# Second heads with queries on partitions in thirteen units instead of eight, value offset 66, four outputs kept in DRAM

## The chip, the cores and the metric

The kernel runs on one core of a Trainium2 chip. The metric is the device time of one execution in microseconds. Before the change three runs took 1343.99 to 1344.94 us, median 1344.91.

A core has TensorE (PE, with weight loads shown apart as PEld), VectorE (DVE), ScalarE (ACT), GpSimd (POOL), SyncE (SP, which here only issues transfers) and 16 DMA engines. Each engine runs its own instructions in order and waits on semaphores for the others.

## The reference

Two layers over 1024 latent tokens and 256 context tokens of width 1024, 16 heads of 64. The first layer is grouped-query attention (four key/value heads, per-head norm and rotary positions on q and k) over all 1280 keys; the second is neighbourhood attention. Each layer's input projection also yields a gate. Cut to what the change touches:

```python
def gqa_axial_mixer(hx, hc, w_in, q_g, k_g, w_out, cos, sin, need_ctx_out):
    ...
    def block(qi):
        s = jnp.einsum('bqkgd,bskd->bkgqs', qi, k_all).astype(jnp.float32) * ATTN_SCALE
        p = jax.nn.softmax(s, axis=-1).astype(v_all.dtype)
        return jnp.einsum('bkgqs,bskd->bqkgd', p, v_all)
    ...
    yx = (o * jax.nn.silu(z)) @ w_out
```

All of it is in float32. The kernel carries float32 operands as two float16 parts (high and low) and makes three products of them: high by high, high by low, low by high.

## The kernel before, in words

**Stages.** First come modulation, norms and the k and v projections (0 to about 95 us). Then the first layer's attention goes over eight pairs of heads. A pair's q and gate projection (`a_proj`) runs about one pair ahead of its attention, in five blocks of two token tiles: `mm` is the 48 matmuls of a block (L1034) with norm, rotation and split, `post` transposes q, `mgen` finds each query's maximum score, `rows` puts the negated maximum into a row of `q2`. Then come the first layer's output projection (`a_out`, L1358), the second layer's pairs (`b_proj`, `b_att`), and its output projection (L1739).

**Two forms of attention.** A unit here is one head of one pair for one half (four tiles) of the latent tokens. There are 32 units; `pt_` 0 and 1 are the halves, and 2 is the context's queries.

- The k form, `a_att`: scores stand with keys on partitions (L1260, L1261), ten tiles of 128x512 a unit. Queries' maxima must be known ahead: `mgen` computes the scores once more, with queries on partitions (L1068 for the latent keys, L1074 for the context), and DVE reduces them (L1069, L1075). ACT takes the exponential twice, to float16 and to float32 (L1245, L1247), `p_split` makes the low part (POOL, every sixth time DVE, L1127 to L1130), and `pv_mm` multiplies by values: three matmuls per tile (L1136 to L1138), whose 65th column sums the probabilities.
- The q form, `q_att`: scores stand with queries on partitions (L1186, L1187), one pass on DVE copies them and takes the maximum (L1190), ACT takes the exponentials (L1202, L1203; the second also sums), and a DMA transpose (L1205) brings the probabilities' two parts to keys on partitions. The products are two matmuls per tile: L1211 multiplies the high part by both value parts, 128 columns, and L1213 the low part by the high values, 64 columns. The two halves of the result are added at the end, and sums are applied by DVE (L1222 to L1229). No `mgen` is needed.

Before the change the q form serves the second head of pairs 0 to 3, in both halves: `QH = range(0, 4)`, eight units. The other 24 have the k form.

**Values.** `v1` (and `bv1` in the second layer) holds, per key tile and head, 130 float16 numbers: 64 high parts, a constant for the sums at 64, 64 low parts from 65, one unused. L1137 and, in the second layer, L1648 read the low parts, `65:129`.

**Buffers.** `y_tile` gives tiles of two rotating sets of four, Y0 and Y1. Outputs `oa` of pairs 0 to 3 stay in Y0, of pairs 4 to 7 in Y1. The q form's probabilities and their transposes (`qpp`) rotate in Y1 too, so they can be there only while pairs 4 and on have no output yet. The output projection's buffers (`opool`) lie where those of the q projection (`aj`) were. The output weights lie where the normed tokens (`xh`) were.

**Order.** Generators with start and end times in units of a pair (`timeline`) write the program's order. Then `Planner` builds the graph of all instructions, gives each a cost per engine, schedules them by list, refines five times with due times and fixes each engine's order. It computes no results; a price in it changes orders alone. DMA transfers are issued by SP in its order.

Of the kernel before, what the change touches and what calls it, by code (L numbers as in the profile page):

```python
# [36 lines left out]
QH = range(0, 4)  # L37
# [5 lines left out]
class Planner:  # L43
# [72 lines left out]
    def cost(self, x, rd, wr):  # L116
# [173 lines left out]
    def schedule(self, key=None, margin=0.0, scale=None):  # L290
# [65 lines left out]
        while count < N:  # L356
# [43 lines left out]
            if e == "PE":  # L400
# [55 lines left out]
    def deadlines(self, margin):  # L456
# [4 lines left out]
        for a in self.order["PE"]:  # L461
            idle += max(0.0, start[a] - prev)
            prev = max(prev, start[a] + (cst[a][0] if tuple(self.node[a].tile_size or (128, 128))[1] == 128
                                         else cst[a][0] / 4))
# [35 lines left out]
def timeline(items):  # L500

    live = [[g, float(a), (float(b) - a) / tot, 0.0] for g, a, b, tot in items]
    while live:
        it = min(live, key=lambda e: e[1] + e[2] * e[3])
        try:
# [4 lines left out]
            live.remove(it)  # L510

# [12 lines left out]
def trunk_kernel(ctx, tc, x, cx, cc, norm_g, ng_row, b_cols, sel_c, w_m0, w_mb, b_mod, a_wkv, a_wq, a_qg, a_kg, a_w_out,  # L524
# [242 lines left out]
    v1 = ap.tile([P, NT, NKV, 130], F16, name="v1")  # L767
# [240 lines left out]

    FTAG = ("pj", "pj", "st", "pj", "pj")

    def a_proj(u, at):
# [3 lines left out]
        def mm(b):  # L1015
            wt = wa[u]
            pt_ = b // 2
            if b % 2 == 0:
# [4 lines left out]
                     [aq.tile([P, 4, 3], F32, name=f"mxp{u}{pt_}{i}", tag=f"mxp{i}", bufs=3) if i == 0 or pt_ == 2 or u not in QH  # L1023
                      else None for i in range(2)])
                if pt_ < 2 and u in QH:
# [34 lines left out]
        def mgen(b):  # L1060
            q1, _, _, mxs = pairs[(u, b // 2)]
            g = u // 2
            for i in ((0,) if b < NX // 2 and u in QH else (0, 1)):
# [14 lines left out]
        def rows(pt_):  # L1078
            q2, mxs = pairs[(u, pt_)][1], pairs[(u, pt_)][3]
            n = PTN[pt_]  # L1080
            for i in ((0,) if pt_ < 2 and u in QH else (0, 1)):
# [7 lines left out]
        for b in range(NT // 2):  # L1089
            m = (1100 if u in QH else 2200) if b < 4 else 440  # L1090
            if u == 0:
                v, w, vp, vm, mw = FIRST[b]
            else:
                v = at + 0.2 * b
                d = 0.2 * (b in (0, 2))
                w, vp, vm, mw = 0.2, v + 0.29 + d, v + 0.31 + d, 0.2 * m / (1100 if u in QH else 2200)
            items.append((mm(b), v, v + w, 5120))
            items.append((post(b), vp, vp + 0.01, 220))
            items.append((mgen(b), vm, vm + mw, m))
            if b in (1, 3, 4):  # L1100
                items.append((rows(b // 2), vm + mw + 0.01, vm + mw + 0.02, 400))
# [30 lines left out]
    def pv_mm(pv, hi, lo, v, n, first, last):  # L1132

        for t in range(n):
            c = slice(t * P, (t + 1) * P)
            T.matmul(pv[:, t, :], hi[:, c], v[:, 0:65], start=first and t == 0, stop=False)  # L1136
            T.matmul(pv[:, t, 0:HD], hi[:, c], v[:, 65:129], start=False, stop=False)  # L1137
# [15 lines left out]

    og_t, og_n = {}, {}
# [6 lines left out]
    def og_done(u, pt_):  # L1161

        og_n[(u, pt_)] = og_n.get((u, pt_), 0) + 1
        if og_n[(u, pt_)] == 2:
            og = og_t[(u, pt_)]
            if pt_ < 2:
                o_out(aq, og, 4, o_dst("oa", oa, u)[:, 4 * pt_:4 * pt_ + 4], u, f"{u}{pt_}")
            else:
                o_out(aq, og, 2, oc[:, u], u, f"{u}c")

    def q_att(u, pt_):
# [5 lines left out]
        sums = aq.tile([P, 4, 3], F32, name=f"qsm{u}{pt_}", tag="qsm", bufs=2)  # L1177
        og = og_of(u, pt_)
        for t in range(4):
# [17 lines left out]
            for c, (k0, n) in enumerate(KCH):  # L1197
# [5 lines left out]
                S.activation(pf, pf, AF.Exp, bias=nmx, accum_out=sums[:, t, c:c + 1])  # L1203
# [3 lines left out]
                def pvs(ppt=ppt, k=k, k0=k0, t=t):  # L1207
                    for x_ in range(k):
                        kt = k0 // P + x_
                        vv = v1[:, kt, g, :].rearrange("p (a b) -> p a b", b=65)[:, :, 0:HD]  # L1210
                        T.matmul(pv[:, t, :].rearrange("p (a b) -> p a b", b=HD), ppt[:, x_], vv,  # L1211
                                 start=t == 0 and kt == 0, stop=False)
                        T.matmul(pv[:, t, 0:HD], ppt[:, k + x_], v1[:, kt, g, 0:HD], start=False,  # L1213
# [7 lines left out]
        sm = aq.tile([P, 4], F32, name=f"qse{u}{pt_}", tag="qse", bufs=2)  # L1221
        V.tensor_reduce(sm, sums, axis=AX.X, op=ALU.add)  # L1222
        V.tensor_scalar_mul(sm, sm, 2.0 * WS * WS)
        V.reciprocal(sm, sm)
        qo = aq.tile([P, 4, HD], F32, name=f"qoc{u}{pt_}", tag="qoc", bufs=1)
# [7 lines left out]
    def a_att(u, pt_):  # L1233
# [19 lines left out]
        for i in ((0,) if pt_ < 2 and u in QH else (0, 1)):  # L1253
# [591 lines left out]
```

## Time and profile before

| | |
|---|---|
| median of three runs | 1344.91 us |
| profiled execution | 1345.52 us |
| its span, first to last instruction | 1343.7 us |
| mean granted TensorE clock | 0.992 |
| first layer's pairs and output projection | about 95 to 785 us |
| second layer's pairs | about 820 to 1288 us |

The profile is of one execution. A row of a group gives line, engine, operation, output and inputs by the program's names, shapes and count, then busy time, the mean ns of one, and the idle time before. Matmuls overlap, so the mean ns of one is longer than what it costs; the timeline shows the starts. Windows give, for each stretch, its length, each engine's busy time with its count of instructions, the granted clock, the DMA engines' busy share and GB/s. A row of a transfer gives size and time from issue to landing.

### The profile page before, as it was taken

What the parts mean: (1) busy time and instruction counts of PE and PEld (TensorE: products, weight loads), DVE (VectorE), ACT (ScalarE), POOL (GpSimd) and SP (SyncE); (2) the same over time, 40 slices, a digit from 0 to 9 for tenths busy, and PEclk for the clock granted to TensorE, in tenths of its full rate; (3) what the DMA queues carried; (4) which work ended last, traced back from release to release, by engine and by line L of the source; (5) the groups of instructions that cost most, each with busy time, mean ns of one, the idle gap of its engine ahead of it and who ended that gap; (6) DMA issues with size and microseconds to landing.
All of it is one profiled execution on the core that took longest, in us unless ns stands there. A gap on an engine that the chain in (4) does not pass through costs nothing.

```text
span 1343.7 us, 38645 instructions
## 1 busy us (share of the span) xinstructions
PE 1309.6 (97%) x15100; PEld 928.6 (69%) x15100; DVE 1067.1 (79%) x2456; ACT 969.0 (72%) x2076; POOL 891.2 (66%) x1214
## 2 busy tenths in 40 slices
PE   8999999999999999999999989999999999999996
PEld 4457777777777777776654457869687786968552
DVE  5898787888889787769528997878888888887665
ACT  4554889988888777798743456878878888887453
POOL 2323878777777767687876467677676868767543
PEclk9899999999999999999999999999999999999998
DMA  9633576786675222244317962678777877669952
GB/s 371 188 116 96 111 152 117 145 187 135 140 145 122 74 67 72 59 119 108 113 51 187 243 139 82 125 145 152 150 139 142 158 143 162 145 151 226 286 130 110
DMA packets 390496, 191.64 MB, mean 143 GB/s; under 512 B 349792, under 2 KB 355104, under 8 KB 390312
## 3 DMA queue, kind: packets, MB, share of 16 engines
q1 hardware_dynamic: 389736, 189.13, 62.1%
q8 instruction: 118, 1.93, 0.6%
q14 instruction: 66, 0.54, 0.1%
q10 hardware_dynamic: 576, 0.03, 0.0%
HBM read 91.03 MB, written 15.75 MB: 79 GB/s over the span
## 4 chain that ended last, share of the span: by engine, by line
PE 73%; DVE 10%; ACT 6%; DMA 5%; issue 3%; POOL 2%; DVEq 0%; POOLq 0%; SPq 0%; ACTq 0%
PE pa L1034 13%; PE poa L1358 6%; PE pob L1739 6%; PE st L1260 3%; PE st L1261 3%; PE pm L1068 3%; PE pkv L887 2%; PE pv L1137 2%; PE pv L1138 2%; PE pv L1136 2%; DMA bpht<-bph 2%; DMA qpp<-qpp 2%; PE pvc L1577 1%; PE qpv L1211 1%; PE pbc L1527 1%
## 5 line engine op out<-in xcount | busy, mean ns | idle before, releaser
L1130 POOL TENSOR_TENSOR pl<-pf,ph 128x256 f16<-128x256 f32 x400 | 274.9, 711 | 85.7 <-ACT pf L1247 56.2
L1130 POOL TENSOR_TENSOR bph<-bpf,bph 128x256 f16<-128x256 f32 (+1 forms) x224 | 184.0, 848 | 102.0 <-ACT bpf L1637 81.8
L1034 PE MATMUL pa<-wa,x 128*128 128x256 f16 x1536 | 219.8, 272 | 0.7 <-DVE q L822 0.7
L1245 ACT ACTIVATE ph<-st 128x512 f16<-128x512 f32 x240 | 143.8, 602 | 58.0 <-PE st L1261 56.2
L1565 PEld LDWEIGHTS <-hx 128*128 128x128 f16 x2688 | 157.3, 98 | 10.2 <-issue 1.3
L1034 PEld LDWEIGHTS <-x 128*128 128x128 f16 x1536 | 140.4, 97 | 33.3 <-issue 1.4
L1247 ACT ACTIVATE pf<-st 128x512 f32<-128x512 f32 x240 | 143.6, 604 | 2.0 <-DVE pl L1127 0.9
L1069 DVE TENSOR_REDUCE mxp<-pm 128x1 f32<-128x512 f32 x192 | 127.3, 683 | 12.8 <-PE pm L1068 11.7
L1137 PE MATMUL pv<-v,ph 128*128 128x64 f16 x960 | 122.4, 195 | 0.0
L1136 PE MATMUL pv<-v,ph 128*128 128x65 f16 x960 | 121.9, 193 | 0.2 <-ACT ph L1245 0.2
L1138 PE MATMUL pv<-v,pl 128*128 128x65 f16 x960 | 121.3, 192 | 0.0
L1130 POOL TENSOR_TENSOR qpp<-qpf,qpp 128x256 f16<-128x256 f32 (+1 forms) x158 | 93.4, 616 | 31.6 <-ACT qpf L1203 29.3
L1517 PEld LDWEIGHTS <-wb 128*128 128x128 f16 x672 | 63.9, 98 | 71.9 <-issue 6.6
L1635 ACT ACTIVATE bph<-bpf,bnx 128x384 f16<-128x384 f32 (+1 forms) x128 | 69.3, 581 | 52.4 <-DVE bnx L1627 33.8
L1136 PEld LDWEIGHTS <-ph 128*128 128x128 f16 x960 | 90.9, 97 | 22.1 <-ACT ph L1245 0.7
L1137 PEld LDWEIGHTS <-ph 128*128 128x128 f16 x960 | 90.4, 97 | 15.8 <-issue 0.4
L1138 PEld LDWEIGHTS <-pl 128*128 128x128 f16 x960 | 91.2, 99 | 9.3 <-POOL pl L1130 1.2
L1260 PE MATMUL st<-q,k 128*128 128x512 f16 x240 | 90.8, 379 | 0.7 <-ACT pf L1247 0.4
L1261 PE MATMUL st<-q,k 65*128 65x512 f16 x240 | 91.5, 381 | 0.0
L1358 PE MATMUL poa<-woa,oa 128*128 128x512 f16 x384 | 89.8, 379 | 0.0
L1739 PE MATMUL pob<-wob,obf 128*128 128x512 f16 x336 | 80.5, 379 | 1.9 <-DVE acc L1742 1.4
L1434 POOL TENSOR_TENSOR wtb<-wsb 128x256 f32<-128x256 f32 x64 | 56.5, 884 | 32.5 <-DMA wsb<-in_b_wp 17.0
(485 smaller groups left out, 4050.2 us busy)
## 6 DMA issues: line engine op xcount, KB each, us to landing
wg<-in_w_mb SPq DMA_DIRECT2D x32, 512.0 KB, 4.5
wsb<-in_b_wp SPq DMA_DIRECT2D x64, 256.0 KB, 2.8
wm<-in_w_m SPq DMA_DIRECT2D x16, 512.0 KB, 9.0
wsa<-in_a_wq SPq DMA_DIRECT2D x32, 256.0 KB, 3.5
xstage<-in_x SPq DMA_DIRECT2D x8, 512.0 KB, 5.6
wsoa<-in_a_w_out SPq DMA_DIRECT2D x16, 256.0 KB, 2.7
x<-in_x SPq DMA_DIRECT2D x8, 512.0 KB, 8.5
x_d<-x SPq DMA_DIRECT2D x8, 512.0 KB, 5.1
```

Of the source, the lines that this page charges most:

```text
L1034: T.matmul(ps[:, :, i, :], hA(a, kt, t), wt[w][:, kt, :], start=n == 0, stop=n == 3 * KT - 1)
L1130: G.tensor_tensor(lo[:, c], p32[:, c], hi[:, c], op=ALU.subtract)
L1136: T.matmul(pv[:, t, :], hi[:, c], v[:, 0:65], start=first and t == 0, stop=False)
L1137: T.matmul(pv[:, t, 0:HD], hi[:, c], v[:, 65:129], start=False, stop=False)
L1138: T.matmul(pv[:, t, :], lo[:, c], v[:, 0:65], start=False, stop=last and t == n - 1)
L1245: S.activation(ph, st, AF.Exp)
L1247: S.activation(p32, st, AF.Exp)
L1260: T.matmul(so, k1[:, g, kc], q1[:, :, i, :], start=True, stop=False)
L1261: T.matmul(so, k2[0:65, g, kc], q2[0:65, :, i, :], start=False, stop=True)
L1358: T.matmul(ps, lhs(a, kt), w[b][:, kt, :], start=n == 0, stop=n == 3 * KT - 1)
L1565: T.matmul(ps[:, t * P:(t + 1) * P], hx[a][:, t, blk, kt], wt[j][:, s_, w, kt], start=first and t == 0 and m == 0, stop=last and t == 3 an ...
L1739: T.matmul(ps, ob[kt][:, t, a], wout["b"][hf][b][:, kt, :], start=n == 0, stop=n == 3 * len(kts) - 1)
```

## The change

- The q form serves the second head of pairs 0 to 6 in the first half and of pairs 0 to 5 in the second half: thirteen units for eight. The predicate is `in_q(u, pt_)`.
- In the q form the products are three matmuls per tile as in the k form, 65, 64 and 65 columns, the sums come from the 65th column, and `o_evict` writes the result. The accumulator of the second exponential and the steps L1222 to L1229 are gone.
- All `oa` tiles are of Y0. Those of pairs 0 to 3 are stored to DRAM (`oa_d`) after their second half and loaded into Y1 (`oa_back`) at 6.98, just ahead of the output weights.
- The rows of values are 132 long, and low parts start at 66.
- Pair 7's projection is spread by a table `LATE` from 6.0 to 7.33, before 6.0 to 7.0. The maxima of its second head follow apart from those of its first.
- In the planner the least price of a matmul is 30.4 ns, 140 for float32 with under 8 columns, and a matmul on 32 columns of the array occupies PE for 0.3 of its cost.

```diff
-QH = range(0, 4)
+QH = (7, 6, 0)
...
-            return max(cols * passes / 2.4 + 2.5, 29.0), 170.0
+            return max(cols * passes / 2.4 + 2.5, 140.0 if f32 and cols < 8 else 30.4), 170.0
...
-                    t[e] = s + 7
+                    t[e] = s + 0.3 * occ
...
+def in_q(u, pt_):
+    return u < QH[pt_]
...
-    v1 = ap.tile([P, NT, NKV, 130], F16, name="v1")
+    v1 = ap.tile([P, NT, NKV, 132], F16, name="v1")
...
-        V.tensor_tensor(v1[:, t, :, 65:129], vv, v1[:, t, :, 0:HD], op=ALU.subtract)
+        V.tensor_tensor(v1[:, t, :, 66:130], vv, v1[:, t, :, 0:HD], op=ALU.subtract)
...
-            d[u] = y_tile((P, NX, 2, P), F16, f"{kind}{u}", u // 4)
+            d[u] = y_tile((P, NX, 2, P), F16, f"{kind}{u}", 0)
...
+    LATE = ((0.0, 0.25, 0.5, 0.66, 0.1, 0.9), (0.3, 0.25, 0.64, 0.76, 0.1, 1.0), (0.7, 0.25, 1.1, 1.3, 0.05, 1.45), (0.97, 0.23, 1.28, 1.36, 0.05, 1.52), (1.1, 0.2, 1.34, 1.38, 0.05))
...
+        late = u == NPAIR - 1
+
+        def heads(pt_):
+            return (0,) if in_q(u, pt_) or late and pt_ < 2 else (0, 1)
...
+            elif late:
+                v, w, vp, vm, mw = (z + at * (n in (0, 2, 3)) for n, z in enumerate(LATE[b][:5]))
...
+            if late and b < 4:
+                vm = at + LATE[b][5]
+                items.append((mgen(b, (1,)), vm, vm + mw, 1100))
+                if b % 2:
+                    items.append((rows(b // 2, (1,)), vm + mw + 0.01, vm + mw + 0.02, 400))
...
-            T.matmul(pv[:, t, 0:HD], hi[:, c], v[:, 65:129], start=False, stop=False)
+            T.matmul(pv[:, t, 0:HD], hi[:, c], v[:, 66:130], start=False, stop=False)
...
+    oa_d = dram.tile([NPAIR // 2, P, NX * 2 * P], F16, name="oa_d")
+
+    def oa_back():
+        for u in range(NPAIR // 2):
+            oa[u] = y_tile((P, NX, 2, P), F16, f"oar{u}", 1)
+            DM.dma_start(oa[u].rearrange("p t a q -> p (t a q)"), oa_d[u])
...
+                if pt_ and u < NPAIR // 2:
+                    DM.dma_start(oa_d[u], oa[u].rearrange("p t a q -> p (t a q)"))
...
-                S.activation(pf, pf, AF.Exp, bias=nmx, accum_out=sums[:, t, c:c + 1])
+                S.activation(pf, pf, AF.Exp, bias=nmx)
...
-                        vv = v1[:, kt, g, :].rearrange("p (a b) -> p a b", b=65)[:, :, 0:HD]
-                        T.matmul(pv[:, t, :].rearrange("p (a b) -> p a b", b=HD), ppt[:, x_], vv,
-                                 start=t == 0 and kt == 0, stop=False)
-                        T.matmul(pv[:, t, 0:HD], ppt[:, k + x_], v1[:, kt, g, 0:HD], start=False,
+                        T.matmul(pv[:, t, 0:65], ppt[:, x_], v1[:, kt, g, 0:65], start=t == 0 and kt == 0, stop=False)
+                        T.matmul(pv[:, t, 0:HD], ppt[:, x_], v1[:, kt, g, 66:130], start=False, stop=False)
+                        T.matmul(pv[:, t, 0:65], ppt[:, k + x_], v1[:, kt, g, 0:65], start=False,
...
-        S.copy(qo, pv[:, :, HD:P])
-        V.tensor_tensor(qo, pv[:, :, 0:HD], qo, op=ALU.add)
-        for t in range(4):
-            V.scalar_tensor_tensor(og[:, t, HD:P], qo[:, t], sm[:, t:t + 1], sz[:, t, HD:P], op0=ALU.mult, op1=ALU.mult)
+        o_evict(aq, pv, og, 4, sz, 0, 1, f"q{u}{pt_}")
...
+    items.append((once(oa_back), 6.98, 6.99, 1))
...
-        v1_ = bq.tile([P, NT, 2, 130], F16, name=f"bv1{u}", tag="v1")
+        v1_ = bq.tile([P, NT, 2, 132], F16, name=f"bv1{u}", tag="v1")
...
-                                T.matmul(pv[:, t % 4, 0:HD], pht[:, x_], v1_[:, kt, i, 65:129], start=False, stop=False)
+                                T.matmul(pv[:, t % 4, 0:HD], pht[:, x_], v1_[:, kt, i, 66:130], start=False, stop=False)
```

More of the change, by code (lines that the diff above doesn't have):

```diff
@@ L1058, in post, with mgen @@
             yield 220
-        def mgen(b):
+        late = u == NPAIR - 1
+        def heads(pt_):
+            return (0,) if in_q(u, pt_) or late and pt_ < 2 else (0, 1)
+        def mgen(b, ii):
             q1, _, _, mxs = pairs[(u, b // 2)]
             g = u // 2
-            for i in ((0,) if b < NX // 2 and u in QH else (0, 1)):
+            for i in ii:
                 if b < NX // 2:
@@ L1076, in mgen, with rows @@
                 yield 220
-        def rows(pt_):
+        def rows(pt_, ii):
             q2, mxs = pairs[(u, pt_)][1], pairs[(u, pt_)][3]
             n = PTN[pt_]
-            for i in ((0,) if pt_ < 2 and u in QH else (0, 1)):
+            for i in ii:
                 zm = zmax[nrow[0] % len(zmax)]
@@ L1252, in a_att @@
         og = og_of(u, pt_)
-        for i in ((0,) if pt_ < 2 and u in QH else (0, 1)):
+        for i in ((0,) if in_q(u, pt_) else (0, 1)):
             pvs = ps_pv(f"pv{u}{i}{pt_}")
@@ L1313, in trunk_kernel @@
     for u in range(NPAIR):
[L1314 removed]
+        for pt_, v, c in ((0, u, 16800 - 8000 * in_q(u, 0)), (1, u + PSH, 16800 - 8000 * in_q(u, 1)), (2, u + 2 * PSH, 2400)):
             items.append((a_att(u, pt_), v, v + (PSH if pt_ < 2 else 1 - 2 * PSH), c))
[L1316 removed]
+            if in_q(u, pt_):
                 items.append((q_att(u, pt_), v - QLEAD, v + PSH - QLEAD, 4 * 1925 + 500))
```

25 lines of the change are left out of this document (9 added, 16 removed).

## The prediction

> **What bounds the kernel now.** I read the page's busy line and its chain first.
>
> ```profile
> span 1343.7 us, 38645 instructions
> PE 1309.6 (97%) x15100; PEld 928.6 (69%) x15100; DVE 1067.1 (79%) x2456; ACT 969.0 (72%) x2076; POOL 891.2 (66%) x1214
> PE 73%; DVE 10%; ACT 6%; DMA 5%; issue 3%; POOL 2%; DVEq 0%; POOLq 0%; SPq 0%; ACTq 0%
> ```
>
> PE is busy for 97% of the span and is 73% of the chain that ended last. A share of busy time is a mean over stages, so the second view is the windows. I cut them where every 240th matmul of the first layer's projection (L1034) starts, because a pair has 240 of them. The first row below is for those matmuls alone and shows one pair's 240. The others are for all instructions, with PE, PEld, DVE, ACT and POOL busy, granted clock and DMA share.
>
> ```profile
> 478.80:553.20 74.40, 36.44 (x240) 21.38 (x240) 1.00 0.29 67
> ...
> 192.20:262.90 70.70, 69.65 (x911) 54.40 (x910) 59.41 (x175) 64.45 (x151) 54.78 (x85) 1.00 0.73 140
> 262.90:332.90 70.00, 68.50 (x868) 52.61 (x865) 59.38 (x169) 61.20 (x144) 51.36 (x78) 1.00 0.77 159
> 332.90:401.50 68.60, 68.24 (x849) 52.31 (x849) 58.53 (x163) 57.62 (x137) 53.05 (x84) 1.00 0.72 145
> 401.50:478.80 77.30, 76.78 (x1044) 58.40 (x1043) 62.80 (x145) 62.90 (x133) 55.05 (x83) 1.00 0.40 91
> 478.80:553.20 74.40, 74.34 (x1011) 56.33 (x1010) 55.33 (x118) 55.61 (x112) 53.21 (x76) 1.00 0.29 67
> 553.20:624.40 71.20, 71.20 (x943) 54.36 (x942) 58.54 (x120) 58.95 (x120) 54.30 (x75) 1.00 0.33 91
> 624.40:690.00 65.60, 64.14 (x775) 38.40 (x773) 33.45 (x70) 48.99 (x95) 52.69 (x73) 1.00 0.34 97
> 690.00:820.00 130.00, 125.54 (x884) 69.13 (x881) 110.43 (x168) 55.74 (x102) 79.72 (x88) 0.99 0.69 168
> 820.00:1288.00 468.00, 462.21 (x5925) 349.06 (x5923) 382.92 (x873) 367.16 (x788) 335.35 (x438) 1.00 0.79 161
> ```
>
> The three windows from 192.2 to 401.5 have the second head with queries on partitions. They last 70.7, 70.0 and 68.6 us, mean 69.8. The three from 401.5 to 624.4 do not, and last 77.3, 74.4 and 71.2, mean 74.3. PE is busy for nearly all of every one, at a granted clock of 1.00, and so it is in the second layer (820 to 1288). ACT is next, at 55 to 64 us. So both attention stages are paid in PE time: what an edit is worth there is how long PE's stream becomes, as long as ACT, DVE, POOL and DMA keep up. Five more units (a unit is one head, half the tokens, one pair) take the form of the shorter windows, where two units are of that form. The windows alone say (74.3 - 69.8) / 2 = 2.3 us a unit, 11.3 us for five, stalls included.
>
> **The change part by part.** A matmul's own duration is no price: matmuls overlap. The price is the distance from one start to the next in the timeline of PE.
>
> ```profile
> 251.26 0.27 PE L1034 MATMUL pa<-wa,xc_hi 128*128 128x256 f16 x1
> 251.37 0.27 PE L1034 MATMUL pa<-wa,xc_lo 128*128 128x256 f16 x1
> ...
> 251.54 0.19 PE L1136 MATMUL pv<-v,ph 128*128 128x65 f16 x1
> 251.57 0.19 PE L1137 MATMUL pv<-v,ph 128*128 128x64 f16 x1
> 251.61 0.19 PE L1138 MATMUL pv<-v,pl 128*128 128x65 f16 x1
> 251.64 0.19 PE L1136 MATMUL pv<-v,ph 128*128 128x65 f16 x1
> 251.66 0.20 PE L1137 MATMUL pv<-v,ph 128*128 128x64 f16 x1
> 251.70 0.19 PE L1138 MATMUL pv<-v,pl 128*128 128x65 f16 x1
> 251.73 0.19 PE L1136 MATMUL pv<-v,ph 128*128 128x65 f16 x1
> ...
> 252.00 0.38 PE L1186 MATMUL qs<-k,q 128*128 128x512 f16 x1
> 252.22 0.22 PE L1211 MATMUL qpv<-v,qpp 128*128 128x128 f16 x1
> 252.28 0.19 PE L1213 MATMUL qpv<-v,qpp 128*128 128x64 f16 x1
> 252.30 0.22 PE L1211 MATMUL qpv<-v,qpp 128*128 128x128 f16 x1
> ...
> 252.56 0.38 PE L1187 MATMUL qs<-k,q 65*128 65x512 f16 x1
> 252.78 0.19 PE L1136 MATMUL pv<-v,ph 128*128 128x65 f16 x1
> ```
>
> So 512 columns take 0.22 us, 256 take 0.11, 128 take 0.06. From 251.54 to 252.00 stand five triples of value products: 92 ns each. From 252.22 to 252.56 stand four pairs of the other form: 85 ns each. Within the triples L1137, with 64 columns, takes about 35 ns, while L1136 and L1138, with 65, take 30 or less; L1213, also 64 columns, takes 20 to 30. L1137 reads from element 65 of a row of 130 two-byte values, an odd place. The others start at an even one.
>
> ```profile
> L1137 PE MATMUL pv<-v,ph 128*128 128x64 f16 x960 | 122.4, 195 | 0.0
> L1138 PEld LDWEIGHTS <-pl 128*128 128x128 f16 x960 | 91.2, 99 | 9.3 <-POOL pl L1130 1.2 <-issue 0.5
> L1648 PE MATMUL bpv<-bv,bpht 128*128 128x64 f16 x608 | 69.1, 195 | 0.0
> L1203 ACT ACTIVATION_READ_ACCUMULATOR qpf<-qpf,qnx 128x1 f32 x96 | 19.2, 200 | 0.0
> oa<-oo SPq DMA_TRANSPOSE x14, 3.1
> acc<-x_d SPq DMA_DIRECT2D x8, 512.0 KB, 6.4
> x<-in_x SPq DMA_DIRECT2D x8, 512.0 KB, 8.5
> ```
>
> *Maxima of five units go.* A unit's maximum pass is 8 matmuls of 512 columns, 4 of 256 and 4 of 128 (the row of maxima): 8 x 0.22 + 4 x 0.11 + 4 x 0.06 = 2.44 us. Five units: -12.2 us. The scores cost the same in either form: twice 10 x 512 columns a unit. The DVE reductions go too, and a pass over the scores that also takes the maximum comes instead; DVE is at 55 to 63 us in windows of 68 to 77 and stays beside PE.
>
> *Value products of the q form: three instructions for two.* The 320 tiles that had this form go from 85 ns to a triple of 30 + 30 + 28 = 88: +1.0 us. The 200 tiles of the moved units go from 92 to 88: -0.8 us. Together about 0.
>
> *Value offset 66 and row 132.* It touches L1137 in what stays of the k form (19 units x 40, and 64 for the context: 824) and L1648 of the second layer (608): 1432 matmuls. If odd starts are the cause, each goes from about 34 to about 29: 1432 x 5 ns = -7.2 us. The ends are 0 (something else makes L1137 slow) and 1432 x 6 = -8.6. I take -7.2, since the only thing in which L1213 differs that should matter is the start.
>
> *ACT and DVE of the q form.* The accumulator reads (19.2 us in all) and a copy and six small DVE operations a unit go; a reciprocal and two multiplications come. All lies beside PE: 0. Were that cover gone, it would be a gain of some 2 us a unit.
>
> *Stalls that the q form brings.* Time less PE busy is 1.05, 1.50 and 0.36 in its windows, mean 0.97, against 0.52, 0.06 and 0.00, mean 0.19: 0.4 us a unit, +2.0 us for five. The moved units issue 12 transposes each on SP, 24 a pair as in the earlier windows, whose DMA share of 0.72 to 0.77 and whose SP queue bear it; so pairs 4 and 5 go from about 0.3 to that.
>
> *Outputs via DRAM.* Four stores and four loads of 512 KB, at about 6.4 us each (row of acc). A store on SP waits for its transpose to land (3.1 us); behind it on SP are weight loads and transposes with buffers ahead. Four such waits, 12 us spread over 280: 0. The loads wait until the last probabilities of pair 6 give up their buffers. They are due 0.42 of a pair (29 us) ahead of the first output projection and take 4 x 6.4 = 26 us if one after another: just covered, 0. Uncovered, the price is up to 26 us. Nothing excludes that it shifts other transfers for the better by the 1.5 us that PE idles from 624 to 690.
>
> *Last pair stretched.* About 2.5 of its five projection blocks (48 x 0.11 = 5.3 us each) and two of its maximum units go from pair 6's window to pair 7's. Pair 6 then has 71.2 - 13 - 5 = 53 us of PE work, against ACT's 58.95 less 2.9 for those blocks, 56. So up to 3 us of stall there unless PE draws on later work; in pair 7 PE gets 82 us against ACT's 52 and stays the bound. Ends 0 and +3, and as a gain the 1.5 us of idle time that is there; I take +2, near the upper end, since the row of pair 6 shows no slack to give. With each block go its ACT and DVE steps, a power on POOL behind the splits of probabilities there, and a transpose and copies on SP, now among the loads of output weights. The output projection's buffers lie where the projection's were, so its residual rows (8.5 us) come only after the last block; the two PSUM banks give PE 10 us of output products meanwhile (2 x 24 x 0.22) and attention fills the rest: 0.
>
> *Planner's prices.* They only change orders. The second layer idles 5.8 us in 468, so a better order can win at most that, and a worse one lose about as much: 0.
>
> Sum: -12.2 - 7.2 + 2.0 + 2.0 = -15.4. The profiled execution took 1345.5 us (span 1343.7), 0.6 above the median of the runs. So 1345.5 - 15.4 = 1330.1, and as a median about 1329.5 us.
>
> **Rivals.** *The offset does nothing.* L1137 would be slow because its weights are those of L1136 again. For it: the same repetition stands in L1648. Against it: it would have to spare the other loads. Time: 1329.5 + 7.2 = about 1337.
>
> *The read-back comes late.* Its place is the start of the output projection near 640 us. The four loads sit on SP in order, ahead of output weights and residual rows, behind buffers that pair 6 must give up. If these buffers come free when PE already needs the tiles, PE waits: four loads one after another, 26 us, less what attention of pair 7 fills. From 15 us of exposed wait the change is slower than before; at the full 26 it ends at 1355. For it: the next 54 us of PE are output projection alone. Against it: 29 us of lead, and loads overlap on 16 DMA engines at a share of 0.34 there.
>
> *Weight loads bind the third product.* Each of the three loads its own weights, and the loads' row says 99 ns. If that could not hide, 320 tiles would pay 99 ns more, 32 us, and the time would be about 1369 with the offset gone too. Against it: three products with three loads take 92 ns together, at 251.54 to 252.00, so loads overlap. The Trainium skill states for such streams, in "TensorE: Matmul & The Clock Gate", section "Back-to-back issue gap", about 81 ns per 128-column matmul with its load; by that the 320 tiles would pay 26 us, and with no gain from the offset the sum would be 1363, slower. The trace disagrees: 92 ns for three.
>
> *The orders and the stretched pair eat the gain.* If pairs 4 to 7 idle as the passage between the layers does (4.5 us in 130) and the second layer doubles its 5.8, some 13 us go: within 0.2% of before, 1343.
>
> **How the numbers follow.** Forecast 0.68; offset without effect 0.16, still faster; orders eat the gain 0.04; late read-back 0.11; weight loads 0.01. A measurement tells from no change what differs by over 0.2%, here 2.7 us. Faster 0.84, same 0.04, slower 0.12. The likeliest case runs from -12.2 - 8.6 - 1.5 with no new stall (1322.6) to 1332.5 with all of pair 6's and twice the stalls of the q form. The range goes 2.6 lower for better orders, and above it takes in the rival at 1337 with 3 us of worse ones: 1320 to 1340, which leaves out late read-back and most of what the orders eat.
>
> **What would show it.** L1068 count 152 for 192 and L1108 108 for 128; pair windows of 68 to 71 us for pairs 4 and 5, with ACT near 60 and a DMA share of 0.7; the start after each L1137 and L1648 coming 28 to 30 ns later; second layer shorter by about 3 us; no PE wait that names the read-back tiles. Wrong it becomes if PE waits on DMA at the first output projection, if pairs 6 and 7 together last longer than their PE work, or if the 64-column products keep their 34 ns.

## The result and the profile after

The changed kernel takes 1353.73 us (median of five runs, 1352.31 to 1360.46) against 1344.91 before: a ratio of 1.0072, 95% interval 1.0049 to 1.0095. It is 9 us slower where 15 us faster was forecast. The profiled execution took 1354.29 us. The first lines of its page:

```profile
span 1352.5 us, 39348 instructions
PE 1304.3 (96%) x15360; PEld 922.4 (68%) x15360; DVE 1071.8 (79%) x2523; ACT 970.2 (72%) x1987; POOL 893.8 (66%) x1235
```

PE is busy 5.3 us less than before, in a span that is 8.8 us longer. Its work did fall; what grew is the time in which it stands still. The windows show where. First the kernel before, then the changed one, in the first layer's attention: window, length, then PE, PEld, DVE, ACT and POOL busy, granted clock, DMA share and GB/s.

```profile
95.00:406.00 311.00, 306.30 (x3740) 237.85 (x3738) 261.73 (x731) 254.07 (x590) 222.49 (x339) 1.00 0.67 137
406.00:551.00 145.00, 144.82 (x1980) 109.78 (x1979) 112.65 (x245) 112.03 (x233) 104.53 (x153) 1.00 0.34 77
551.00:695.00 144.00, 142.54 (x1797) 98.05 (x1795) 94.07 (x196) 112.16 (x222) 110.81 (x152) 1.00 0.33 92
```

```profile
95.00:406.00 311.00, 302.65 (x3977) 234.24 (x3976) 242.98 (x674) 241.44 (x485) 219.70 (x338) 0.99 0.73 140
406.00:551.00 145.00, 140.38 (x1939) 107.27 (x1936) 113.78 (x322) 119.79 (x238) 107.20 (x164) 1.00 0.77 148
551.00:695.00 144.00, 137.08 (x1768) 94.02 (x1767) 104.03 (x229) 112.58 (x225) 110.61 (x159) 1.00 0.55 129
```

PE's idle time in the three goes from 4.7, 0.2 and 1.5 us (together 6.35) to 8.4, 4.6 and 6.9 (19.9): 13.5 us more. The first window holds the value products of the same seven and a half units of the q form in both kernels, the second about four of the new ones, the third the last. So 3.7 of the 13.5 us came where no unit is new. What PE waits for in this stretch, before and after (who waited for what: us in total, times, longest):

```profile
PE qpv L1211 <- DMA qpp<-qpp: 0.9, 2, 0.7
```

```profile
PE qpv L1237 <- DMA qpp<-qpp: 9.3, 16, 1.5
PE st L1278 <- ACT pf L1265: 4.2, 7, 1.8
PE pm L1079 <- issue: 2.1, 1, 2.1
```

The first value product of the q form now waits for the transpose of its probabilities. The scores of the k form wait until ACT has read the buffer that they go to.

These waits count only gaps that the modelled ends of matmuls leave open. A finer measure is the distance from each start of PE to the next, less the median for a matmul of its line and form, where it is longer than that; added up I call it stall. From 95 to 695 us the stall is 32.7 us before and 50.9 after.

A small part of this is the clock. Here is one window before and after (the clock is the third number from the end):

```profile
263.00:335.00 72.00, 70.50 (x892) 54.42 (x889) 61.01 (x177) 63.20 (x149) 53.46 (x82) 1.00 0.78 160
```

```profile
263.00:335.00 72.00, 69.37 (x924) 52.45 (x921) 56.66 (x160) 56.66 (x113) 51.14 (x78) 0.98 0.86 160
```

An estimate of its worth is 0.02 of 72 us, 1.4 us of the 18.2. Over the whole execution the clock was 0.994 in this profile and 0.992 before, so it does not explain the 9 us.

The matmuls of the first layer's output projection, before and after, with first and last start (the last two numbers):

```profile
L1358 PE MATMUL poa<-woa,oc x96: 378/380/380, 753.5 to 774.0; 128*128 128x512 f16 x96
```

```profile
L1376 PE MATMUL poa<-woa,oar x192: 377/379/380, 646.0 to 756.5; 128*128 128x512 f16 x192
L1376 PE MATMUL poa<-woa,oc x96: 379/379/379, 759.3 to 779.8; 128*128 128x512 f16 x96
```

The first layer ends 5.8 us later (779.8 for 774.0). From there to PE's last start it is 558.7 us before and 562.4 after: the second layer loses another 3.7, though in its instructions nothing changed but the place of the low parts.

### The profile page after: what moved, and what is told of

The parts are those of the page before. It is cut to its first block, busy times and chain, and to the rows that moved or that the text cites. A ratio compares the mean times of both kernels' runs of the same rounds, so it can differ in the third digit from the quotient of the medians.

```text
span 1352.5 us, 39348 instructions
## 1 busy us (share of the span) xinstructions
PE 1304.3 (96%) x15360; PEld 922.4 (68%) x15360; DVE 1071.8 (79%) x2523; ACT 970.2 (72%) x1987; POOL 893.8 (66%) x1235
## 5 line engine op out<-in xcount | busy, mean ns | idle before, releaser
L1149 POOL TENSOR_TENSOR pl<-pf,ph 128x256 f16<-128x256 f32 x322 | 221.9, 712 | 51.5 <-ACT pf L1265 47.7
L1149 POOL TENSOR_TENSOR qpp<-qpf,qpp 128x256 f16<-128x256 f32 (+1 forms) x254 | 150.7, 618 | 59.9 <-ACT qpf L1230 41.3
L1263 ACT ACTIVATE ph<-st 128x512 f16<-128x512 f32 x190 | 112.8, 606 | 38.1 <-PE st L1279 35.5
L1229 ACT ACTIVATE qpp<-qpf,qnx 128x512 f16<-128x512 f32 x156 | 99.0, 653 | 35.1 <-DVE qnx L1223 25.2
L1265 ACT ACTIVATE pf<-st 128x512 f32<-128x512 f32 x190 | 114.3, 611 | 0.6 <-DVE pl L1146 0.3
L1217 DVE CUSTOM_DVE_ANT_0 qpf<-qs,zero 128x512 f32<-128x512 f32 x156 | 92.9, 598 | 27.0 <-POOL qpp L1149 15.8
L1230 ACT ACTIVATE qpf<-qpf,qnx 128x512 f32<-128x512 f32 x156 | 98.6, 650 | 0.8
L1654 ACT ACTIVATE bph<-bpf,bnx 128x384 f16<-128x384 f32 (+1 forms) x128 | 69.3, 582 | 39.7 <-DVE bnx L1646 30.8
L1155 PE MATMUL pv<-v,ph 128*128 128x65 f16 x760 | 94.7, 193 | 0.0
L1156 PE MATMUL pv<-v,ph 128*128 128x64 f16 x760 | 94.3, 194 | 0.0
L1157 PE MATMUL pv<-v,pl 128*128 128x65 f16 x760 | 94.0, 192 | 0.3 <-POOL pl L1149 0.3
L1155 PEld LDWEIGHTS <-ph 128*128 128x128 f16 x760 | 71.5, 97 | 14.4 <-ACT ph L1263 0.8
L1156 PEld LDWEIGHTS <-ph 128*128 128x128 f16 x760 | 71.1, 97 | 9.6
```

The source lines that it names most:

```text
L1149: G.tensor_tensor(lo[:, c], p32[:, c], hi[:, c], op=ALU.subtract)
L1156: T.matmul(pv[:, t, 0:HD], hi[:, c], v[:, 66:130], start=False, stop=False)
L1157: T.matmul(pv[:, t, :], lo[:, c], v[:, 0:65], start=False, stop=last and t == n - 1)
L1229: S.activation(ph, pf, AF.Exp, bias=nmx)
L1230: S.activation(pf, pf, AF.Exp, bias=nmx)
L1263: S.activation(ph, st, AF.Exp)
```

## The experiments

All ratios are to the kernel before on the same chip, with 95% intervals; its median there was 1344.3 to 1346.4 us.

**The offset alone.** Rows of 132 and low parts from 66 in the kernel before, in both layers; the order of every engine stays the same. Of the edit, two lines of the first layer:

```diff
-    v1 = ap.tile([P, NT, NKV, 130], F16, name="v1")
+    v1 = ap.tile([P, NT, NKV, 132], F16, name="v1")
...
-            T.matmul(pv[:, t, 0:HD], hi[:, c], v[:, 65:129], start=False, stop=False)
+            T.matmul(pv[:, t, 0:HD], hi[:, c], v[:, 66:130], start=False, stop=False)
...
```

> The kernel before with rows of values 132 long and low parts from 66, nothing else; all five engines keep their order. Theory now (the start of the low parts is not what makes the 64-column product slow: in the changed kernel it still takes 33 ns to the next start): 1344.9 us, within 1.5, and 33 ns again. Rival (the prediction's: an odd start costs 5 ns, and the changed kernel loses it elsewhere): 7 us less, 1337.7, and 28 to 29 ns.

1344.86 us, ratio 0.999 (0.998 to 1.0). The 64-column product takes 33 ns to the next start, as before. The -7.2 us of the sum are not there.

**The prices alone, and the change without them.** Three lines of the planner, put into the kernel before; and the changed kernel with these three as they were.

```diff
-            return max(cols * passes / 2.4 + 2.5, 29.0), 170.0
+            return max(cols * passes / 2.4 + 2.5, 140.0 if f32 and cols < 8 else 30.4), 170.0
...
-                    t[e] = s + 7
+                    t[e] = s + 0.3 * occ
...
-                                         else cst[a][0] / 4))
+                                         else cst[a][0] * 0.3))
```

> The kernel before with the planner's three new prices, nothing else: only orders change. Theory (the new prices make worse orders: the second layer lost 4 us between the kernels with no work of its own changed but the offset): 3 to 6 us more, 1348 to 1351. Rival (orders differ only by chance, within 2 us; the loss comes with the new units): 1343 to 1347.

1354.14 us, ratio 1.0070 (1.0044 to 1.0096), above both expected ranges. The same work takes as long as the changed kernel.

> The changed kernel with the planner's old prices. If the prices cost time: 3 to 6 us less than the changed kernel, 1348 to 1351. If they do not: within 2 us of 1353.7. The waits of the first value product of the q form on its transposes (9.3 us in the changed kernel) stay if they come with the units, and go if they come with the prices.

1355.44 us, ratio 1.0069 (1.0051 to 1.0088). Taking the prices out again brings nothing. The wait for the transposes was 6.3 us, less than the changed kernel's 9.3, but it did not go. So prices alone lose all of the 9 us, and all the rest alone loses them too. Two causes that add would not do that; one good thing that either destroys would.

**The stretched pair.** The changed kernel with the projection of pair 7 in its old place.

```diff
-        late = u == NPAIR - 1
+        late = False
```

> The changed kernel with pair 7's projection in its old place (6.0 to 7.0). Theory A (stretching starves PE in pairs 6 and 7, where the idle time of PE grew most): 4 to 8 us less, 1346 to 1350, and PE idle under 3 us from 551 to 640. Theory B (idle time comes from the q form's transposes and the number of units): within 2 us of 1353.7, or more, if the stretched blocks were the only work to cover those waits.

1354.4 us, ratio 1.0066 (1.0042 to 1.0089): theory B. The table `LATE` neither costs nor brings what can be measured.

**Another order of the same work.** The suspicion was now that the kernel before stands on a good order that any edit gives up. The planner's margin is a safety distance in its own accounts. Altered by a nanosecond or two it changes no computation (PE has 15100 matmuls at each margin in the work of before, 15360 in the changed work), only the order. Done for both kernels:

```diff
-        plan.schedule(margin=100.0)
-        plan.refine(5, 100.0, 300.0)
+        plan.schedule(margin=101.0)
+        plan.refine(5, 101.0, 300.0)
```

> The kernel before with the planner's margin 101 ns for 100, a change that means nothing but writes another order. Theory (the kernel before stands on a lucky order, some 7 us under what its work gives on average, and any new order gives that up): 1349 to 1355 us. Rival (orders differ by 2 us at most, and the new prices are bad by themselves): 1344 to 1348.

> The changed kernel with the planner's margin 101 ns for 100. Theory of orders: anywhere from 1348 to 1358, so that one order says little of the change. Rival (the changed kernel's loss is of its work and waits, whatever the order): 1352 to 1356, with PE's waits for the transposes of the q form (9.3 us) within 2 us of that.

> The kernel before with the planner's margin 98 ns: another order of the same work. Theory (its own order is a good one among many): 1349 to 1356. Rival (the two slower orders so far were bad ones): 1343 to 1348.

> The kernel before with the margin 102 ns. As for 98: theory 1349 to 1356, rival 1343 to 1348.

> The changed kernel with the margin 102 ns. If the five units' stalls are what eats their gain, in any order: 1352 to 1359, like its other orders. If the changed kernel's work is worth 10 us or more in some orders: under 1348.

> The changed kernel with the planner's margin 98 ns. Theory (over orders the two works take the same time within 2 us, since the five units bring as much stall as they spare): 1352 to 1358, mean of four margins 1354 to 1356 against 1351.6 for the kernel before with its own order in and 1353.7 without it. Rival (the changed work is faster in most orders): under 1350.

| margin | work of before: us, ratio | changed work: us, ratio |
|---|---|---|
| 98 | 1354.71, 1.0078 (1.0059 to 1.0098) | 1353.63, 1.0055 (1.0034 to 1.0075) |
| 100 (as written) | 1344.91, 1 | 1353.73, 1.0072 (1.0049 to 1.0095) |
| 101 | 1352.63, 1.0046 (1.0028 to 1.0065) | 1356.59, 1.0084 (1.0068 to 1.0100) |
| 102 | 1353.94, 1.0074 (1.0057 to 1.0091) | 1353.74, 1.0074 (1.0057 to 1.0091) |

This settles it as far as three other orders of each can. The work of the kernel before takes 0.46 to 0.78% longer in each of three other orders, mean 0.66%. The changed work takes 0.55 to 0.84% longer, mean 0.71%. The kernel with the prices alone is a fourth other order of the old work (0.70%), the one without the stretched pair nearly the changed work again (0.66%). Between the two works there is no difference that these runs can tell. The 9 us are what the kernel before has from its own order.

The attention windows of the profiles (95 to 695 us; kernel before with margins 98, 101 and 102) show a part of that:

```profile
95.00:695.00 600.00, 588.21 (x7407) 439.49 (x7405) 462.08 (x1161) 473.80 (x1034) 432.14 (x635) 0.99 0.53 111
```

```profile
95.00:695.00 600.00, 589.89 (x7483) 443.42 (x7481) 462.45 (x1166) 478.09 (x1040) 437.14 (x641) 1.00 0.53 111
```

```profile
95.00:695.00 600.00, 589.04 (x7445) 442.04 (x7444) 470.50 (x1166) 476.82 (x1038) 436.55 (x639) 1.00 0.52 111
```

PE idles for 11.8, 10.1 and 11.0 us there, against 6.35 in the order as written. And the changed work, with margins 98, 101 and 102:

```profile
95.00:695.00 600.00, 581.02 (x7696) 438.39 (x7694) 463.86 (x1231) 474.35 (x947) 440.29 (x659) 1.00 0.69 140
```

```profile
95.00:695.00 600.00, 579.07 (x7664) 435.80 (x7662) 455.72 (x1227) 474.33 (x944) 440.33 (x657) 0.99 0.69 140
```

```profile
95.00:695.00 600.00, 584.45 (x7749) 439.28 (x7747) 461.21 (x1232) 476.54 (x950) 441.67 (x663) 1.00 0.70 140
```

19.0, 20.9 and 15.6 us, and 19.9 as written: mean 18.8 against 11.0 for the other orders of the old work. By starts, the stall is 49 us on the mean of the four, against 39 for the three: 10 us more for the change. Each figure is of one profiled execution, and those with margin 101 are off their medians (1348.01 for 1352.63, 1359.84 for 1356.59). Without these two, and with the run of the prices alone as a third order of the old work, it is 48 against 41. So the change brings 7 to 10 us of stall in these orders. It spares about 12 us of maxima and pays 2 for its value products; the stall eats most or all of the rest.

**Eight units in the changed kernel.**

```diff
-QH = (7, 6, 0)
+QH = (4, 4, 0)
```

> The changed kernel with eight units of the q form, pairs 0 to 3, and all the rest of it: new prices, DRAM, stretched last pair, three products. Theory (five more units bring as much stall as they take work: 12 us of maxima against about that of waits): 1352 to 1357, as with thirteen, PE work up by 12 and stalls down by 10 to 14. Rival (more units are a gain and the other parts lose it): 1360 to 1367. Second rival (more units are a loss in all): 1344 to 1349.

1356.54 us, ratio 1.0077 (1.0057 to 1.0098): as with thirteen. The profiled execution is the slowest of its four (1359.45 us). In it the first layer ends at 785.4 us against 779.8, but 3.1 of these 5.6 us lie ahead of the attention, whose first projection starts at 95.4 for 92.3. The stall from 95 to 695 us is 41.5 against 50.9. So the five units spare 12 us of PE work, bring 9 of stall, and leave about 3, which the medians (1356.5 and 1353.7, one order each) do not resolve.

**Two products for three.** The changed kernel with the old value products of the q form, and its sums by the accumulator.

```diff
-                        T.matmul(pv[:, t, 0:65], ppt[:, x_], v1[:, kt, g, 0:65], start=t == 0 and kt == 0, stop=False)
-                        T.matmul(pv[:, t, 0:HD], ppt[:, x_], v1[:, kt, g, 66:130], start=False, stop=False)
...
+                        T.matmul(pv[:, t, :].rearrange("p (a b) -> p a b", b=HD), ppt[:, x_], vv,
+                                 start=t == 0 and kt == 0, stop=False)
...
```

> The changed kernel with the old two products a tile of the q form and its accumulated sums. By starts, two products take 86 ns and three 93, so PE's work falls by 520 x 7 ns = 3.6 us; ACT gets 156 accumulator reads back, 31 us over eight pairs. Theory (PE's work and stalls add): 1349 to 1352. Rival (ACT stands beside PE no longer, because the q form's chain is what PE waits for): no gain, 1353 to 1358.

1357.57 us, ratio 1.0073 (1.0047 to 1.0099). The 3.6 us do not show; within the spread of orders that is no proof either way.

**What the q form waits for.** Two tries to take its waits away. First, the planner believes that a transfer lands later, so that it puts value products further back.

```diff
-                fin = dma + 1500
+                fin = dma + 3500
```

> The changed kernel with one price of the planner altered: a transfer lands 3500 ns after its share of the queue, before 1500. Theory (PE stands still before value products of the q form because the planner believes that their transposes have landed): those waits fall from 9.3 us to under 3, and the time by 5 to 9, to 1345 to 1349. Rival (transposes are late because SP and the DMA engines can't bring them sooner; a later place in the order only moves the wait): waits go over to other products, time within 3 us of 1353.7.

1354.96 us, ratio 1.0072 (1.0055 to 1.0089). The waits of PE from 95 to 695 us now:

```profile
PE st L1278 <- ACT pf L1265: 1.9, 3, 1.0
PE qpv L1237 <- DMA qpp<-qpp: 1.8, 4, 0.8
PE qs L1213 <- DVE mxp L1086: 1.7, 4, 0.9
PE pv L1155 <- DVE og L1137: 1.3, 2, 1.1
PE pmc L1085 <- ACT q L1128: 1.2, 2, 0.7
PE pm L1079 <- DVE mxp L1080: 1.1, 2, 0.6
PE qs L1213 <- DVE qmx L1217: 1.1, 2, 0.5
```

The wait for transposes falls from 9.3 to 1.8 us, and waits for DVE and ACT take its place; the stall is 47 us for 51, within what other orders of this work have (45 to 52). The time does not move. The rival came true: taking this wait away moved it to other products. In this order, then, the late transposes are the form in which the stall shows; that they are not its cause in others is not shown.

Second, a wider ring. The 256-key chunk gets a buffer of its own, and the room comes from one of the five buffers of the k form's low parts; the control has only that buffer less.

```diff
-            pl = aq.tile([P, 512], F16, name="pl" + nm, tag="pl", bufs=5)
+            pl = aq.tile([P, 512], F16, name="pl" + nm, tag="pl", bufs=4)
...
-                pq = y_tile((P, 2, 8, P), F16, f"qpp{nm}{c}", 1)
+                pq = (y_tile((P, 2, 8, P), F16, f"qpp{nm}{c}", 1) if c < 2 else
+                      aq.tile([P, 2, 4, P], F16, name=f"qpp{nm}{c}", tag="qpx", bufs=1))
```

> The changed kernel in which the 256-key chunk of the q form's probabilities has a buffer of its own, so that the ring of four in Y1 holds two tokens' tiles of chunks and not one and a third; the room comes from the k form's low parts (four buffers for five). Theory (the ring bounds the q form: a chunk holds its buffer from the exponential to the last product, and 13 units need it in every window): PE's waits for the q form's transposes and scores, together 13 us of start-to-start stall for products and 4 for scores, fall by half, and the time by 6 to 9, to 1345 to 1348. Rival (four are enough, the chain is bound elsewhere): stalls within 3 us, time 1350 to 1358.

> The changed kernel with four buffers for the k form's low parts, nothing else: the control for the run with the wider ring. Expected by both: within 3 us of 1353.7, since POOL makes them well ahead of PE; if it is 1358 or more, that run is read against this one.

The control takes 1359.83 us (1.0095, 1.0070 to 1.0120), the wider ring 1367.41 (1.0155, 1.0133 to 1.0177), outside both expected ranges. With it PE still waits for the transposes, 9.0 us in the control and here:

```profile
PE qpv L1238 <- DMA qpp<-qpp: 11.9, 17, 2.5
```

The waits did not fall by half, so the theory of the ring falls. The kernel is also slower for another reason: from the end of the first layer to PE's last start it takes 574.2 us, where the other kernels take 557 to 567 for the same work. So an order, it seems, can cost more than 10 us in a stage that an edit does not touch. The control came out 6 us above 1353.7, twice the 3 that were expected.

**What makes the 64-column product slow.** One kernel with three forms of it: in the k form rows of 136 with the low parts from 72, in the q form the 64 columns as the third product of a tile, and in the second layer (the last edit shown) 65 columns from 66.

```diff
-                        T.matmul(pv[:, t, 0:HD], ppt[:, x_], v1[:, kt, g, 66:130], start=False, stop=False)
-                        T.matmul(pv[:, t, 0:65], ppt[:, k + x_], v1[:, kt, g, 0:65], start=False,
+                        T.matmul(pv[:, t, 0:65], ppt[:, k + x_], v1[:, kt, g, 0:65], start=False, stop=False)
+                        T.matmul(pv[:, t, 0:HD], ppt[:, x_], v1[:, kt, g, 72:136], start=False,
...
-                                T.matmul(pv[:, t % 4, 0:HD], pht[:, x_], v1_[:, kt, i, 66:130], start=False, stop=False)
+                                T.matmul(pv[:, t % 4, 0:65], pht[:, x_], v1_[:, kt, i, 66:131], start=False, stop=False)
```

> The changed kernel with three forms of the 64-column product, for starts in PE's timeline alone. In the k form the low parts start at 72 of rows of 136, a multiple of 16 bytes. In the q form the 64-column product comes third, after the low probabilities, so that its weights are not those just loaded. In the second layer it has 65 columns, the last of them zero. What makes it slow shows in the one that goes from 33 to 29 ns: start, repeated weights, or width.

Median distances to the next start: k form (start at a multiple of 16 bytes, weights those of the product ahead) 28 ns, q form (such a start, other weights ahead) 28, second layer (start at element 66, not such a multiple, 65 columns, weights repeated) 34. So the start matters for products that repeat the weights, and a 65th column does not help. Whether a start off such a multiple is slow with other weights ahead, this kernel does not test.

The kernel before has a case of that. L1213 multiplies 64 columns from a row's first element, with other weights than L1211 ahead of it. Rows of 130 two-byte values take 260 bytes and the four rows of a key tile 1040, which is a multiple of 16. So the rows of the second key/value head (pairs 2 and 3) start 4 bytes further off a multiple of 16 than those of the first (pairs 0 and 1). At least one of the two groups is off it. From pair 3:

```profile
360.99 0.19 PE L1213 MATMUL qpv<-v,qpp 128*128 128x64 f16 x1
361.02 0.22 PE L1211 MATMUL qpv<-v,qpp 128*128 128x128 f16 x1
361.07 0.19 PE L1213 MATMUL qpv<-v,qpp 128*128 128x64 f16 x1
361.10 0.22 PE L1211 MATMUL qpv<-v,qpp 128*128 128x128 f16 x1
```

L1211 follows L1213 after 28.2 to 28.7 ns on the mean in each of the eight units. A start off a multiple of 16 bytes is thus not enough to make a product slow. All that were slow also repeat the weights of the product ahead; that it takes both fits every trace here, but no run parts the two.

The single run took 1347.85 us, in an order of its own. Two kernels that keep their orders follow up the start.

```diff
-    v1 = ap.tile([P, NT, NKV, 132], F16, name="v1")
+    v1 = ap.tile([P, NT, NKV, 136], F16, name="v1")
...
-            T.matmul(pv[:, t, 0:HD], hi[:, c], v[:, 66:130], start=False, stop=False)
+            T.matmul(pv[:, t, 0:HD], hi[:, c], v[:, 72:136], start=False, stop=False)
```

> The changed kernel with rows of 136 and low parts from 72 in the first layer; all engines keep its order. Theory (low parts that start at a multiple of 16 bytes take about 2 ns less a tile of three products, as the starts showed in one look): 1344 products' tiles at 2.2 ns, 3 us less, 1350 to 1352. Rival (PE waits for the chain of the q form anyway and gives the time back there): within 1 us of 1353.7.

1351.14 us, ratio 1.0062 (1.0037 to 1.0086), for the changed kernel's 1353.73 and 1.0072. The two were measured against different medians of the kernel before, and by the ratios the gain is about 1.3 us; the intervals overlap, so the time does not show it. Here is a stretch of the timeline of PE, first of the changed kernel, then of this one:

```profile
697.87 0.19 PE L1156 MATMUL pv<-v,ph 128*128 128x64 f16 x1
697.90 0.19 PE L1157 MATMUL pv<-v,pl 128*128 128x65 f16 x1
697.93 0.19 PE L1155 MATMUL pv<-v,ph 128*128 128x65 f16 x1
697.96 0.20 PE L1156 MATMUL pv<-v,ph 128*128 128x64 f16 x1
698.00 0.19 PE L1157 MATMUL pv<-v,pl 128*128 128x65 f16 x1
```

```profile
640.73 0.20 PE L1155 MATMUL pv<-v,ph 128*128 128x65 f16 x1
640.77 0.19 PE L1156 MATMUL pv<-v,ph 128*128 128x64 f16 x1
640.79 0.19 PE L1157 MATMUL pv<-v,pl 128*128 128x65 f16 x1
640.82 0.19 PE L1155 MATMUL pv<-v,ph 128*128 128x65 f16 x1
640.85 0.19 PE L1156 MATMUL pv<-v,ph 128*128 128x64 f16 x1
640.88 0.20 PE L1157 MATMUL pv<-v,pl 128*128 128x65 f16 x1
```

After L1156 the next start comes 0.03 to 0.04 us later in the first, 0.02 to 0.03 in the second; over all of the k form the means are 32.8 and 29.2 ns. But L1155 goes from 29.9 to 31.8, as at 640.73, so a triple is 1.7 ns shorter (90.2 for 91.9), not 4. The second, in the kernel before and its second layer alone:

```diff
-        v1_ = bq.tile([P, NT, 2, 130], F16, name=f"bv1{u}", tag="v1")
+        v1_ = bq.tile([P, NT, 2, 132], F16, name=f"bv1{u}", tag="v1")
...
-                                T.matmul(pv[:, t % 4, 0:HD], pht[:, x_], v1_[:, kt, i, 65:129], start=False, stop=False)
+                                T.matmul(pv[:, t % 4, 0:HD], pht[:, x_], v1_[:, kt, i, 68:132], start=False, stop=False)
```

> The kernel before with rows of 132 and low parts from 68 in the second layer alone, so at multiples of 8 bytes and, for the second head of a pair, of 16; all engines keep their order. If multiples of 8 are enough: 608 tiles at 2.2 ns, 1.3 us less than the kernel before, and 28 to 30 ns after the 64-column product. If only 16 counts: about half of the products at 28 and the rest at 33, 0.7 us. If the start has nothing to do with it: 33 ns, no change.

1345.12 us, ratio 0.9994 (0.9983 to 1.0005): no measurable gain. The product's distances fall into two groups, mean 30.8 ns: near 33 in each first head of a pair and near 28 in each second, whose low parts start at multiples of 16 bytes. That is as expected if only these count. A version clearly faster than both kernels was not found.

## Why the prediction was wrong

**The bound was read rightly, the slack was not.** PE's work was the first to count: 152 maxima matmuls for 192 and 108 row matmuls for 128, as written, and at PE's median distances (216, 109 and 56 ns for 512, 256 and 128 columns) that is 12.0 us, for the 12.2 forecast. But "as long as ACT, DVE, POOL and DMA keep up" was the weak clause.

**The step that failed most: the planner's prices "only change orders", priced 0 within 5.8 us.** The ends came from idle time of the second layer, as if an order could lose no more than what is idle now. The profile showed one order of the work. It could not show that other orders idle more: 0.46 to 0.78% in three, 9 us on the mean. A low idle time is a property of an order as much as of the work. The rival nearest to the result, "the orders and the stretched pair eat the gain", had the right place and got 0.04, since its price of 13 us was taken from those idle rows too. Missing were 24 us (1353.7 for 1329.5). Roughly, 9 of them are this order, 5 to 8 the stalls of the q form and 7 the value offset.

**Stalls of the q form: +2.0 forecast.** They were read from PE busy, 0.4 us a unit. Busy time uses modelled ends, which cover short gaps: over the same 600 us PE idles 6.35 us by busy time where the stall is 32.7. Against other orders of the old work, the changed work has 8 us more idle time by busy time and 7 to 10 more stall by starts. By starts the changed kernel has 9 us less stall with eight units of the q form than with thirteen: 1.9 us a unit.

**Value offset: -7.2 forecast, 0 measured.** The delay was real (33 ns for 28) and the start has a part in it, but "even" was the wrong rule: the trace of before had only value products that start at a row's first element and at its element 65, and I took the odd number for what sets them apart. L1137 also repeats the weights of L1136, which L1213 does not do with L1211's. The rival "the offset does nothing" (0.16) was right in its price; its reason, the repeated weights, is not the whole, since a start at a multiple of 16 bytes is fast with them, but it is not ruled out as a condition.

**Value products: about 0 forecast, +2.** A tile went from 86 to 92 ns for 320 tiles, since the middle product kept its 33 ns.

**Right:** the read-back is hidden. Its four loads are issued by SP from 604.4 to 613.4 us and first used at 646.0, no wait of PE names them:

```profile
L1178 SPq DMA_DIRECT2D oar<-oa_d x4: 326/342/533, 604.4 to 613.4; - x4
```

That rival (0.11) had the right sign by another road, and the one of weight loads (0.01) is out: three products with three loads take 92 ns. The windows for pairs 4 and 5 are 71.3 and 72.8 us by the projection's starts, just above the 68 to 71 expected. The DMA share there is 0.77, as forecast. The stretched pair's +2 could not be found: with and without, the same time.

**By the sum.** Against the forecast the profile is 24.2 us long. By starts: 14.2 more stall from 95 to 695 us than the 4 allowed (2 for the q form, 2 for the stretched pair), 7.2 of offset, 3.7 of the second layer, 2.1 of the value products, less 3.0 by which the attention began earlier (92.3 for 95.3 us). That is 24.2; what the list leaves out is under 1 us each way and cancels.

**What stays open.** Why the kernel before idles so little in its own order, 6.35 us against 10 to 12, was not found. One wait stands out: for the first value product of the q form, 0.9 us in its own order, and in the other orders of the old work 2.9 to 5.7 (the row is of margin 98):

```profile
PE qpv L1211 <- DMA qpp<-qpp: 4.6, 6, 1.5
```

What in its order avoids this wait is not known, nor whether that order was chosen for its time. The idle time from 95 to 695 us accounts for about half of its 9 us. What holds up the chain of the q form is open too: neither a later place for its products nor a wider ring helped, and ACT, DVE and SP were not relieved one by one.

## What to carry to other kernels

When a planner or a scheduler writes the order, try a neutral change of it before you judge an edit: here the same work moved by 0.7%, as much as the whole result, and a single pair of times would have blamed the edit. A bound at 97% busy says what an edit may spare; it does not say that the spared time can be had, because the chains beside it have to be served too. Read PE's slack from starts, not from busy time.

## What the runs showed of the hardware

- A 64-column float16 product that repeats the weights of the product ahead is followed 28 ns later when its moving operand starts at a multiple of 16 bytes, counted from the start of its tile, and 33 to 34 ns later at the other starts tried; so is one of 65 columns from element 66 (34 ns). The product ahead gets 2 ns longer when the start is such a multiple, so a tile of three gains 1.7 ns. With other weights ahead, L1213 takes 28 ns from rows of both starts. Why is not known.
- The landing of the q form's transposes took 3.2 us (median) with eight units and 4.0 with thirteen, at a DMA share of 0.51 and 0.70 from 95 to 695 us; in another order with thirteen (margin 102, share 0.70) it took 3.7.
- Three matmuls of 64 and 65 columns, each with a weight load of its own, take 90 to 93 ns together. The Trainium skill's page "TensorE: Matmul & The Clock Gate", section "Back-to-back issue gap", states about 81 ns for each matmul of 128 columns with its load in such streams; the measurements here disagree: L1211, 128 columns and a load of its own, is followed 57 ns later (median, kernel before).
